# A decoder block on one core: the operand steps of the up products, the transposes and the first weight operands stand elsewhere in the program

## The chip, the cores and the metric

The kernel runs on one core of one Trainium2 chip. The metric is the device time of one launch in microseconds (us), as the median of the runs. Before the change it is 2093.09 us (three runs, 2091.72 to 2096.36). The profiled execution is another one: it took 2088.7 us, 2086.9 us from its first to its last instruction.

## What is computed

One layer of a hybrid decoder block over 1040 tokens (16 meta tokens and 1024 real ones) of 1024 channels, in float32. The part that the change touches is the end of the mixer and the start of the gated MLP:

```python
def block(h):
    mix = hybrid_mixer(rms_norm(h, g_pre_mix), ...)      # ends in: merged @ w_out
    h = h + rms_norm(mix, g_post_mix)
    ffn = conv_gated_mlp(rms_norm(h, g_pre_ffn), w_up_gate, conv_w_ffn, w_down)
    return (h + rms_norm(ffn, g_post_ffn))[:, 16:]

def conv_gated_mlp(xn, w_up_gate, conv_w_ffn, w_down):
    u, g = split(xn @ w_up_gate, 2)                      # 1024 x 5632
    u = causal_dwconv(u, conv_w_ffn)
    return (gelu(u) * g) @ w_down
```

So the norm of every token needs its whole row of `merged @ w_out`, and the up product needs the normalised rows with channels on the partitions, which is a transpose.

## The kernel before

Every float32 matmul is made of three passes: an operand is split into a high part (a cast, on ScalarE) and a low part (source less high part, on VectorE or GpSimd), and high x high, high x low and low x high are summed. `split` (L67) makes the two halves of an operand.

**Output projection (L921 to L938).** The tokens go in 9 blocks of 114 (QB), numbered 0 to 8. For each block `out_chunk` makes three chunks of up to 342 columns, 24 matmuls each, in one of three `po` banks (PSUM); ScalarE squares the chunk (L708) and VectorE multiplies it by the gain (L709). `post_block` then makes the first norm's root (`rstd_of`, L71: VectorE, one ScalarE square root, VectorE), the new row of h (L723), its square (L726), the second root and the normalised row xv (L728). Eight TensorE transposes of xv (L735) and two copies out of PSUM (L745 on ScalarE, L747 on VectorE) put the block into `xr`. The transposes of a block are kept in the list `to_transpose` and called after the third chunk of the next block.

**Operands of the up products.** The up product is a fast scheme over 2 x 2 blocks: seven products instead of eight, over token pairs (even tokens E, odd tokens O; the digit is the half of the channels). Its seven data operands are B11 = E1, T1 = O1 - E1, T2 = O2 - T1, B21 = E2, T3 = T2 - E1, B22 = O2 and T4 = E2 - T2, each split into high and low parts; the differences overwrite `xr`. The 514 pairs are worked in two halves (`HALF`: 258 and 256 pairs), because the first half needs only blocks 0 to 4. `x_early` makes B11, T1 and the sums of T2 and T3; `x_late` makes T2, B21, T3, B22 and T4. The low parts of B11, B21 and B22 are made on GpSimd, the others on VectorE. For the first half `x_early(0)` stands in block 6 and `x_late(0)` behind block 8; for the second half both stand behind the sixth product of the first set.

**Up products.** A set of `products` is seven groups of 12 matmuls in the order B11, T1, T2, B21, T3, B22, T4; ScalarE takes three snapshots of unfinished banks (L853, L856, L859), VectorE adds them in `evac_u` (L899). Pair 0 is worked as two sets, one for each half of the tokens (258 and 256 columns), then comes the gate pair as one set of 512 columns, and so on over 22 pairs. The weight operands of a pair (seven, from two raw tiles of 512 KB) come from `prep_pair`: ScalarE cast, GpSimd low part, and three VectorE sums. `prep0` is that of pair 0, `prep` that of the next one.

**Order.** The order in which instructions stand on each engine is set by a scheduler from the written order and from the waits, so it is not quite that of the code; each engine then works its own list strictly in order. The excerpts of the order below are from the built programs. TensorE's list at this joint was B11, T1 (first half), the transposes of block 8, then T2, B21, T3, B22, T4.

In the built program before, the operands are numbered: opB_13038 is B11, opT_13039 T1, opT_14199 T2, opB_14200 B21, opT_14201 T3, opB_14202 B22, opT_14203 T4. In the changed one opT_14168 is T2, opB_14167 B21, opT_14166 T3, opB_14258 B22, opT_14257 T4 (B11 and T1 keep theirs). 128x4x258 is an operand half for the first 258 pairs, 128x4x256 for the second.

## Time and profile before

| | us |
|---|---|
| median of 3 runs | 2093.09 |
| runs | 2091.72 to 2096.36 |
| profiled execution | 2088.7 |
| its span, first to last instruction | 2086.9 |
| TensorE busy | 1988.2 (95% of the span) |
| VectorE busy | 1070.9 (51%) |
| ScalarE busy | 851.7 (41%) |
| GpSimd busy | 908.1 (44%) |

TensorE (PE) is busy nearly throughout; of 40 slices of the span, the first, one from about 1357 us on and the last one fall short of nine tenths. In the timeline a row is the start, the duration, the engine, the line, the operation, what it writes and reads, and how often; in brackets stands how long the engine had been idle before it and what ended that. VectorE is DVE, ScalarE ACT, GpSimd POOL; SPq is the queue that issues transfers. Neighbouring matmuls overlap in the records, so the pace of TensorE is read from start to start.

### The profile page before, as it was taken

The page shows a single profiled execution, that of the slowest core. Times are in us where ns is not written, and L with a number is a line of the kernel's source. Part 1 is how long each engine was busy: PE and PEld are TensorE (multiplying, and loading weights), DVE is VectorE, ACT ScalarE, POOL GpSimd, SP SyncE. Part 2 cuts the span into 40 slices and gives each one's busy share as a digit, 9 for nine tenths or more (in the row PEclk, how much of TensorE's full clock was granted, in tenths as well). Part 3 has the DMA queues.
Part 4 walks back from the last instruction along what each step waited for, and adds up shares of the span by engine and source line. Part 5 has one row for each costly group of instructions (what it writes and reads, how often), then busy time and mean ns, then how long its engine had stood idle before and what let it go on. Part 6 is the DMA issues. An engine that isn't in the chain of part 4 may idle for free. (4 is left out here: it accounts for less than half of the span.)

```text
span 2086.9 us, 30864 instructions
## 1 busy us (share of the span) xinstructions
PE 1988.2 (95%) x12228; PEld 1858.4 (89%) x12228; DVE 1070.9 (51%) x1685; ACT 851.7 (41%) x1769; POOL 908.1 (44%) x765
## 2 busy tenths in 40 slices
PE   5999999999999999999999999969999999999997
PEld 4999999999999999999999999968998898878876
DVE  6455565655555565564341125774435444445547
ACT  4444454545454454544430123354344334321122
POOL 4443444434353444344122560155555655554353
PEclk9999999999999999999999999989999999999999
DMA  3111111111111101111475674302212222243223
GB/s 134 41 51 41 61 31 51 41 51 41 51 51 41 51 31 62 41 51 61 143 229 172 183 184 147 102 30 82 101 62 81 87 76 81 71 174 120 81 81 132
DMA packets 56030, 177.58 MB, mean 85 GB/s; under 512 B 12728, under 2 KB 12728, under 8 KB 55884
## 3 DMA queue, kind: packets, MB, share of 16 engines
q1 hardware_dynamic: 54732, 173.50, 25.7%
q8 instruction: 96, 1.57, 0.3%
q10 hardware_dynamic: 1152, 2.10, 0.3%
q14 instruction: 50, 0.41, 0.1%
HBM read 131.36 MB, written 44.21 MB: 84 GB/s over the span
## 5 line engine op out<-in xcount | busy, mean ns | idle before, releaser
L128 PE MATMUL mm<-xnT,whi 128*128 128x342 f32 (+2 forms) x1536 | 506.6, 330 | 5.1 <-ACT xnT L68 3.6
L129 PE MATMUL mm<-xnT,whi 128*128 128x342 f32 (+2 forms) x1536 | 493.8, 321 | 0.5 <-DVE xnT L69 0.5
L130 PE MATMUL mm<-xnT,wlo 128*128 128x342 f32 (+2 forms) x1536 | 492.2, 320 | 0.0
L338 POOL TENSOR_TENSOR be<-be,fl 114x127 f32<-114x127 f32 (+2 forms) x144 | 176.8, 1228 | 402.6 <-DVE fl L336 195.1
L128 PEld LDWEIGHTS mm<-xnT,whi 128*128 128x128 f32 x1536 | 289.8, 189 | 10.1 <-ACT xnT L68 4.2
L129 PEld LDWEIGHTS mm<-xnT,whi 128*128 128x128 f32 x1536 | 290.4, 189 | 2.1 <-DVE xnT L69 1.0
L130 PEld LDWEIGHTS mm<-xnT,wlo 128*128 128x128 f32 x1536 | 289.7, 189 | 0.0
L69 POOL TENSOR_TENSOR wlo<-raw,whi 128x1024 fp32r<-128x1024 f32 x80 | 205.7, 2572 | 189.9 <-ACT whi L68 189.9
L69 POOL TENSOR_TENSOR a_op<-raw,a_op 128x512 fp32r<-128x512 f32 (+1 forms) x134 | 185.7, 1400 | 96.7 <-ACT a_op L68 94.2
L336 DVE TENSOR_TENSOR_SCAN fl<-fl 114x128 f32<-114x128 f32 (+2 forms) x144 | 205.0, 1423 | 4.9
L69 DVE TENSOR_TENSOR al<-tp,ah 128x342 fp32r<-128x342 f32 (+4 forms) x288 | 126.9, 450 | 139.7 <-ACT ah L68 137.5
L68 ACT CAST ah<-tp 128x342 fp32r<-128x342 f32 (+4 forms) x288 | 113.1, 398 | 189.8 <-PE tp L372 181.9
L844 PE MATMUL st<-opT,a_op 128*128 128x258 f32 (+2 forms) x528 | 172.3, 326 | 15.0 <-DVE owork L899 7.9
L846 PE MATMUL st<-opT,a_op 128*128 128x258 f32 (+2 forms) x528 | 169.7, 321 | 0.0
L848 PE MATMUL st<-opT,a_op 128*128 128x258 f32 (+2 forms) x528 | 169.6, 321 | 0.0
L327 ACT ACTIVATE fl<-z 114x348 f32<-114x348 f32 (+10 forms) x240 | 111.5, 465 | 130.3 <-PE z L326 122.9
L68 ACT CAST a_op<-raw 128x512 fp32r<-128x512 f32 (+1 forms) x134 | 82.9, 628 | 161.5 <-DMA raw<-in_w_up_gate_dram 58.0
L1089 DVE TENSOR_TENSOR acc<-acc,st 128x512 f32<-128x512 f32 x144 | 98.4, 687 | 96.1 <-PE st L1084 96.1
L372 PE MATMUL tp<-ident,be 114*128 114x114 f32 x720 | 119.5, 263 | 25.6 <-DVE al L69 21.0
L846 PE MATMUL st<-opB,a_op 128*128 128x512 f32 (+2 forms) x396 | 127.6, 322 | 1.0 <-POOL opB L69 1.0
L844 PE MATMUL st<-opB,a_op 128*128 128x512 f32 (+2 forms) x396 | 127.4, 322 | 0.0
L848 PE MATMUL st<-opB,a_op 128*128 128x512 f32 (+2 forms) x396 | 127.3, 321 | 0.0
(164 smaller groups left out, 4374.3 us busy)
## 6 DMA issues: line engine op xcount, KB each, us to landing
raw<-in_w_in_dram SPq DMA_DIRECT2D x64, 512.0 KB
raw<-in_w_up_gate_dram SPq DMA_DIRECT2D x44, 512.0 KB
act_d<-owork SPq DMA_DIRECT2D x22, 512.0 KB
araw<-act_d SPq DMA_DIRECT2D x22, 512.0 KB
raw<-in_w_down_dram SPq DMA_DIRECT2D x22, 512.0 KB
y_d<-yy SPq DMA_DIRECT2D x8, 513.0 KB
ga_d<-gt SPq DMA_DIRECT2D x8, 513.0 KB
o_d<-ot SPq DMA_DIRECT2D x8, 513.0 KB
```

Of the source, the lines that this page charges most:

```text
L68: nc.scalar.copy(hi, src)
L69: (lo_engine or nc.vector).tensor_tensor(lo, src, hi.bitcast(F32), op=ALU.subtract)
L128: nc.tensor.matmul(ps, wh, xh, start=(kb == 0), stop=False)
L129: nc.tensor.matmul(ps, wh, xl, start=False, stop=False)
L130: nc.tensor.matmul(ps, wl, xh, start=False, stop=(kb == KB - 1))
L327: nc.scalar.activation(fl[:, c0:c0 + n], z, AF.Sigmoid, scale=-0.125)
L336: nc.vector.tensor_tensor_scan(fl[:, :nk][:, ::-1], fl[:, :nk][:, ::-1], fl[:, :nk][:, ::-1], 1.0, op0=ALU.mult, op1=ALU.min)
L338: nc.gpsimd.tensor_tensor(be[:, 0:nk - 1], be[:, 0:nk - 1], fl[:, 1:nk], op=ALU.mult)
L372: nc.tensor.transpose(tp[:n, QB * j:QB * (j + 1)], blocks[j][0][:, kb * P:kb * P + n], ident[:QB, :QB])
L844: nc.tensor.matmul(ps, wt[:, 0, k], xh, start=start and kb == 0, stop=False, skip_group_check=True)
L846: nc.tensor.matmul(ps, wt[:, 0, k], xl, start=False, stop=False, skip_group_check=True)
L848: nc.tensor.matmul(ps, wt[:, 1, k], xh, start=False, stop=stop and kb == 3, skip_group_check=True)
```

## The change

- The transposes of a block are called after the first chunk of the block after next (before: after the third chunk of the next block), as long as two are waiting. Block 7's transposes come after the second product of the first set, block 8's after the sixth, in the code.
- `x_early` and `x_late` are taken apart into `op_split` and `x_t1` to `x_t4` over ranges of pairs: R0 is the first half, R1 pairs 258 to 398, R2 399 to 513, RL both. For the first half B11, T1 and the sums of T2 and T3 stand in blocks 6 and 7; T2, B21 and T4's sum stand between the last matmuls of block 8 and its evacuation; T3 stands inside `post_block(8)`, in the two places where it waits for ScalarE; B22 and T4 stand after the third product. For the second half B11, and later T1, of R1 stand in block 8 and behind the third product, the rest after the sixth.
- Low parts of B11 (except R0), B21 and B22 (except RL) go from GpSimd to VectorE. Low parts of the merged input `mb` of blocks 6, 7 and 8 go from VectorE to GpSimd.
- The weight operands of pair 0 are asked for in blocks 2 to 5, 7 and 8, their raw tiles in block 0. The weights' low parts stay on GpSimd.
- Memory: `ones_up`, `tmp_s`, one row tile and the operand tiles move between pools; the pool `late` is opened in block 8, and `late2` holds T4 and B22.

```diff
@@ load_m
-        split(t[:, 0], t[:, 1], raw)
+        split(t[:, 0], t[:, 1], raw, nc.gpsimd if b > 5 else nc.vector)
...
@@ post_block
+    def post_block(b, ssq, between=(lambda: None, lambda: None)):
...
         r = rstd_of(osml, s0, QB)
+        between[0]()
         nc.vector.scalar_tensor_tensor(h, h, r, xv, op0=ALU.mult, op1=ALU.add)
...
         nc.scalar.activation(xv, h, AF.Square, accum_out=s2[:QB])
+        between[1]()
         r2 = rstd_of(osml, s2, QB)
...
+    def op_split(name, r, which, engine):
+        t = ops[name][:, :, :, r[0]:r[1]]
+        split(t[:, 0], t[:, 1], quarter(r, which), engine)
...
+    def x_t1(r):
+        sub(nc.vector, quarter(r, "O1"), quarter(r, "O1"), quarter(r, "E1"))
+    def x_t2(r):
+        sub(nc.vector, quarter(r, "O1"), quarter(r, "O2"), quarter(r, "O1"))
+    def x_t3(r):
+        sub(nc.vector, quarter(r, "E1"), quarter(r, "O1"), quarter(r, "E1"))
+    def x_t4(r):
+        sub(nc.vector, quarter(r, "E2"), quarter(r, "E2"), quarter(r, "O1"))
+    R0 = HALF[0]
+    R1, R2 = (258, 399), (399, NJ)
+    RL = (258, NJ)
...
+    def ahead(b, c):
+        if (b, c) == (0, 2):
+            load_pair(0)
+        elif 1 < b < 6 and c == 1:
+            next(prep0)
+        elif b == 6:
+            if c == 1:
+                op_split("B11", R0, "E1", nc.gpsimd)
+                x_t1(R0)
+            elif c == 2:
+                op_split("T1", R0, "O1", nc.vector)
+        elif b == 7:
+            if c == 1:
+                x_t2(R0)
+            elif c == 2:
+                x_t3(R0)
+                next(prep0)
+        elif b == 8:
+            if c == 0:
+                next(prep0)
+            elif c == 1:
+                op_split("B11", R1, "E1", nc.vector)
+                x_t1(R1)
...
         for c in range(3):
-            out_chunk(b, c, sums)
-            if b == 6 and c == 2:
-                x_early(0)
...
-        if to_transpose:
-            to_transpose.pop(0)()
-        post_block(b, sums)
+            ps = out_products(b, c)
+            if (b, c) == (8, 2):
...
+                op_split("T2", R0, "O1", nc.vector)
+                op_split("B21", R0, "E2", nc.vector)
+                x_t4(R0)
+            out_evac(b, c, ps, sums)
+            if c == 0 and len(to_transpose) > 1:
+                to_transpose.pop(0)()
+            ahead(b, c)
...
-        if k >= 1:
-            next(prep0, None)
-        if k == 5:
+        elif k == 1:
             to_transpose.pop(0)()
...
+        elif k == 2:
+            op_split("B22", R0, "O2", nc.vector)
+            op_split("T4", R0, "E2", nc.vector)
+            op_split("T1", R1, "O1", nc.vector)
+        elif k == 5:
+            to_transpose.pop(0)()
+            op_split("B11", R2, "E1", nc.vector)
+            x_t1(R2)
+            op_split("T1", R2, "O1", nc.vector)
+            x_t2(RL)
+            op_split("T2", RL, "O1", nc.vector)
+            op_split("B21", RL, "E2", nc.vector)
+            x_t3(RL)
+            op_split("T3", RL, "E1", nc.vector)
+            op_split("B22", RL, "O2", nc.gpsimd)
+            x_t4(RL)
+            op_split("T4", RL, "E2", nc.vector)
```

VectorE, from the evacuation of block 8's last chunk on, before (tmp_s and raw are the weight sums of pair 1; s, v and t belong to the root):

```order
L709 TENSOR_TENSOR row_13049<-po,g_post 114x340
L747 COPY xr<-tp 128x4x114
L721 TENSOR_REDUCE s_14163<-sums 114x1
L76 TENSOR_SCALAR v<-s_14163 114x1
L78 RECIPROCAL s<-s 114x1
L79 SCALAR_TENSOR_TENSOR t<-s,v 114x1
L80 TENSOR_SCALAR t<-t 114x1
L81 TENSOR_TENSOR s<-s,t 114x1
L723 SCALAR_TENSOR_TENSOR row_13049<-row_13049,s,xv_13047 114x1024
```

VectorE at the same place now:

```order
L712 TENSOR_TENSOR row_13048<-po,g_post 114x340
L770 TENSOR_TENSOR xr<-xr 128x1032
L724 TENSOR_REDUCE s_14177<-sums 114x1
L770 TENSOR_TENSOR opT_14166<-xr,opT_14166 128x4x258
L72 TENSOR_SCALAR v<-s_14177 114x1
L752 COPY xr<-tp 128x4x114
L74 RECIPROCAL s<-s 114x1
L830 TENSOR_TENSOR tmp_s<-raw 128x512
L75 SCALAR_TENSOR_TENSOR t<-s,v 114x1
L770 TENSOR_TENSOR raw<-raw 128x512
L76 TENSOR_SCALAR t<-t 114x1
L770 TENSOR_TENSOR raw<-tmp_s,raw 128x512
```

The step of T4's sum, T3's low part and the three weight sums, which stood ahead of or behind this piece before, now stand inside it, ahead of the new row of h (L727, the second row after these).

ScalarE from the same evacuation on, before (L708 squares the chunk, L77 is the root, L853 to L859 the snapshots):

```order
L708 ACTIVATE row_13049,sums<-po 114x340
L745 COPY xr<-tp 128x4x114
L77 ACTIVATE s<-v 114x1
L853 COPY snap<-st 128x258
L856 COPY snap<-st 128x258
L726 ACTIVATE xv_13047,s_14176<-row_13049 114x1024
```

ScalarE now:

```order
L711 ACTIVATE row_13048,sums<-po 114x340
L983 CAST opT_14166<-xr 128x4x258
L867 COPY snap<-st 128x258
L870 COPY snap<-st 128x258
L750 COPY xr<-tp 128x4x114
L873 COPY snap<-st 128x258
L73 ACTIVATE s<-v 114x1
L730 ACTIVATE xv_13046,s_14191<-row_13048 114x1024
L64 CAST opB_14258<-xr 128x4x258
```

The root of block 8 (L77, now L73) moved behind all three snapshots and behind the copy of block 7's transposes; the high part of B22 stands behind block 8's second root.

TensorE around the transposes of block 8, before:

```order
L848 MATMUL st<-opT_13039,a_op 128x258
L735 MATMUL tp<-ident,xv_13047 128x114 x5
L844 MATMUL st<-opT_14199,a_op 128x258
L735 MATMUL tp<-ident,xv_13047 128x114 x3
L844 MATMUL st<-opB_14200,a_op 128x258
```

TensorE around them now:

```order
L862 MATMUL st<-opT_14166,a_op 128x258
L740 MATMUL tp<-ident,xv_13046 128x114 x5
L858 MATMUL st<-opB_14258,a_op 128x258
L740 MATMUL tp<-ident,xv_13046 128x114 x3
L860 MATMUL st<-opB_14258,a_op 128x258
```

Block 8's transposes moved from behind T1's product to behind T3's; block 7's, which stood ahead of the first product, now stand behind T1's.

## Rows read from the trace of the kernel before

**Rows 1.** The page: span, and busy time of each engine.

```profile
span 2086.9 us, 30864 instructions
PE 1988.2 (95%) x12228; PEld 1858.4 (89%) x12228; DVE 1070.9 (51%) x1685; ACT 851.7 (41%) x1769; POOL 908.1 (44%) x765
```

**Rows 2.** Busy time by stretch: PE, weight loads, DVE, ACT, POOL, clock, DMA.

```profile
1245.00:1357.20 112.20, 107.87 (x699) 106.90 (x698) 72.89 (x154) 42.12 (x109) 16.16 (x10) 0.98 0.39 123
1357.20:1402.50 45.30, 28.51 (x183) 26.72 (x182) 34.68 (x38) 21.71 (x34) 23.42 (x10) 0.77 0.04 11
1402.50:1420.70 18.20, 16.89 (x75) 13.44 (x74) 12.13 (x10) 10.34 (x15) 10.50 (x9) 1.00 0.18 59
```

**Rows 3.** Timeline of TensorE: transposes of blocks 3 to 8, and restarts after waits.

```profile
1304.33 0.95 PE L735 MATMUL tp<-ident,xv 114*128 114x114 f32 x8
1316.40 0.94 PE L735 MATMUL tp<-ident,xv 114*128 114x114 f32 x8
1331.80 1.52 PE L735 MATMUL tp<-ident,xv 114*128 114x114 f32 x8 [2.76 <-DVE xv L728]
1345.02 0.94 PE L735 MATMUL tp<-ident,xv 114*128 114x114 f32 x8
1357.03 0.94 PE L735 MATMUL tp<-ident,xv 114*128 114x114 f32 x8
1367.11 1.19 PE L735 MATMUL tp<-ident,xv 114*128 114x114 f32 x5 [6.25 <-DVE xv L728]
1385.82 0.56 PE L844 MATMUL st<-opT,a_op 128*128 128x258 f32 x1 [4.81 <-DVE owork L899]
1402.71 0.40 PE L844 MATMUL st<-opB,a_op 128*128 128x512 f32 x1
1409.76 0.50 PE L844 MATMUL st<-opT,a_op 128*128 128x512 f32 x1 [1.31 <-ACT snap L853]
```

**Rows 4.** Timeline of TensorE, second token half: the pace at both clocks.

```profile
1389.60 0.41 PE L844 MATMUL st<-opB,a_op 128*128 128x256 f32 x1
1389.82 0.41 PE L846 MATMUL st<-opB,a_op 128*128 128x256 f32 x1
1390.18 0.28 PE L844 MATMUL st<-opT,a_op 128*128 128x256 f32 x1
1390.30 0.28 PE L846 MATMUL st<-opT,a_op 128*128 128x256 f32 x1
```

**Rows 5.** Timelines of ACT and DVE: block 8's chain to xv, a snapshot.

```profile
1357.22 0.46 ACT L708 ACTIVATE row<-po 114x340 f32<-114x340 f32 x1 [3.18 <-PE po L706]
1357.34 0.69 DVE L816 TENSOR_TENSOR tmp_s<-raw 128x512 f32<-128x512 f32 x1 [1.24 <-DMA raw<-in_w_up_gate_dram]
1359.52 0.51 DVE L709 TENSOR_TENSOR row<-po,g_post 114x340 f32<-114x340 f32 x1
1360.85 0.20 ACT L77 ACTIVATE s<-v 114x1 f32<-114x1 f32 x1 [2.65 <-DVE v L76]
1361.92 1.28 DVE L723 SCALAR_TENSOR_TENSOR row<-row,s,xv 114x1024 f32<-114x1024 f32 x1
1365.68 1.28 DVE L728 SCALAR_TENSOR_TENSOR xv<-row,s,g_pre 114x1024 f32<-114x1024 f32 x1
1373.99 0.38 ACT L859 COPY snap<-st 128x258 f32<-128x258 f32 x1 [0.47 <-PE st L848]
```

**Rows 6.** Timelines of DVE and POOL behind it: operand steps alone and side by side.

```profile
1369.91 1.24 DVE L69 TENSOR_TENSOR opT<-xr,opT 128x1032 fp32r<-128x1032 f32 x1 [2.95 <-ACT opT L68]
1371.09 15.96 POOL L69 TENSOR_TENSOR opB<-xr,opB 128x1032 fp32r<-128x1032 f32 x5 [16.76 <-PE tp L735]
1374.56 6.86 DVE L763 TENSOR_TENSOR xr<-xr 128x1032 f32<-128x1032 f32 x2
1384.91 1.09 DVE L899 TENSOR_TENSOR owork<-st,snap 128x258 f32<-128x258 f32 x3
```

**Rows 7.** Timeline of the transfer queue: the second raw tile of pair 1.

```profile
1353.11 0.35 SPq L800 DMA_DIRECT2D raw<-in_w_up_gate_dram  x1
```

More of the change, by code (lines that the diff above doesn't have):

```diff
@@ L673, in block_kernel @@
     ops = {name: early.tile([P, 2, 4, NJ], F32R, name=f"op{name}") for name in ("B11", "T1")}
-    tmp_s = early.tile([P, 512], F32, name="tmp_s")
     o_ctx = ctx.enter_context(ExitStack())
+    osml = o_ctx.enter_context(pool("osml", 4))
     ow = o_ctx.enter_context(pool("ow"))
-    osml = o_ctx.enter_context(pool("osml", 4))
     xvs = [pl.tile([P, D], F32, name=f"xv{i}") for i, pl in enumerate((early, ow))]
-    rws = [ow.tile([P, D], F32, name=f"row{i}") for i in range(2)]
+    rws = [pl.tile([P, D], F32, name=f"row{i}") for i, pl in enumerate((early, ow))]
+    tmp0 = ow.tile([P, 512], F32, name="tmp0")
     g_pre2 = ow.tile([P, D], F32, name="g_pre2")
@@ L808, in prep_pair @@
         got = a_ops[i] = {}
+        if i == 0:
+            tmp_s = tmp0
+        else:
+            tmp_s = shared.get("tmp")
+            if tmp_s is None:
+                tmp_s = shared["tmp"] = mpool.tile([P, 512], F32, name="tmp_s", tag="mb")
         def keep(name, src):
@@ L950, in bank_of @@
+            out_evac(b, c, ps, sums)
+            if c == 0 and len(to_transpose) > 1:
+                to_transpose.pop(0)()
+            ahead(b, c)
+        if b == 8:
+            t3, e1 = ops["T3"][:, :, :, R0[0]:R0[1]], quarter(R0, "E1")
+            post_block(b, sums, (lambda: nc.scalar.copy(t3[:, 0], e1),
+                                 lambda: sub(nc.vector, t3[:, 1], e1, t3[:, 0].bitcast(F32))))
+        else:
+            post_block(b, sums)
     def bank_of(pl, tag):
         return lambda: pl.tile([P, 512], F32, name="st", tag=tag)
-    first = products(0, *HALF[0], bank_of(ps_mm2, "mm"), evac_u(*HALF[0]))
@@ L954, in block_kernel @@
-    for k, _ in enumerate(first):
-        if k >= 1:
-            next(prep0, None)
-        if k == 5:
-            to_transpose.pop(0)()
-            x_early(1)
-            x_late(1)
+    for k, _ in enumerate(products(0, *HALF[0], bank_of(ps_mm2, "mm"), evac_u(*HALF[0]))):
+        if k == 0:
+            next(prep0)
+        elif k == 1:
+            to_transpose.pop(0)()
+            o_ctx.close()
+            late2 = late_ctx.enter_context(pool("late2", 1, "right"))
+            for name in ("T4", "B22"):
+                ops[name] = late2.tile([P, 2, 4, NJ], F32R, name=f"op{name}")
+        elif k == 2:
[15 more added lines that the diff above has]
+            op_split("T4", RL, "E2", nc.vector)
```

62 lines of the change are left out of this document (20 added, 42 removed).

## The prediction

> **What bounds the kernel now.** Read the page first: TensorE is busy for 95% of the span, no other engine for more than 51% [rows 1]. So a change of the order can only win where TensorE waits or runs slowly, and the stretches are compared next: through the output projection it is busy for 107.87 of 112.20 us at a clock of 0.98, but from there to the gate pair for 28.51 of 45.30 us at 0.77, and in the gate pair at 1.00 again [rows 2]. The change touches just these. Then the timeline of TensorE tells where the time goes [rows 3].
>
> Between undisturbed blocks transposes follow each other after 1316.40 - 1304.33 = 12.07 us. From 1316.40 to 1345.02, two blocks, it is 28.62 instead of 24.14: **4.5 us** lost. The wait itself is 2.76 us, for xv of block 5; the rest is the slow restart (eight transposes in 1.52 us instead of 0.94).
>
> I call 0 the moment at which block 8's last chunk ends (1357.03, where the transposes of block 7 begin). The gate pair begins at 1402.71, so at **45.7**. What must run in between is two sets of 84 matmuls at 0.12 us [rows 4], 20.2 us, and twice eight transposes, 1.9 us: 22.1. So **23.6 us** are lost, and two waits show why: 6.25 us for xv of block 8, then 4.81 us at VectorE's additions; after both the pace is 0.22 us a matmul instead of 0.12, which ends 4.2 us after the restart at 1385.82 (0.22 from 1389.60 to 1389.82, 0.12 from 1390.18 on) [rows 3, 4]. Last, 1.31 us in the gate pair, for a snapshot [rows 3].
>
> Why VectorE is late is in its own timeline: an operand step of 1032 elements takes 1.24 us alone and 6.86 / 2 = 3.43 us while GpSimd makes the B operands, five in 15.96 us, 3.2 each [rows 6].
>
> **The change part by part.**
>
> *Transposes a chunk later, operand steps of the first half spread.* A chunk is (12.07 - 0.94) / 3 = 3.7 us. Block 5's xv was 2.76 us late; its transposes are now asked for 3.7 us later, and in VectorE's list only one of the four long steps of the first half stands ahead of this xv. I take the whole 4.5 us; the ends are 0 and 4.5, since the same VectorE work stays in this block.
>
> *Reload of xv.* Its row tile is free a chunk later, so the transfer starts a chunk later. It has two chunks and the first root, about 10 us, and a 512 KB tile took 1353.11 to 1357.34, 4.2 us, from issue to use [rows 5, 7]: hidden, with some 6 us to spare. In the transfer queue only these reloads change places.
>
> *Weights of pair 0 in early blocks; mb on GpSimd.* As many instructions as before; VectorE is busy for 72.89 of these 112.20 us and GpSimd for 16.16 [rows 2]. That cover hides them: 0. What it costs without the cover is the first rival.
>
> *First half after block 8.* B11 and T1: 24 x 0.12 = 2.9; block 7's transposes to 3.8; T2, B21 and T3, 36 x 0.12 = 4.3, to 8.1. Their low parts stand in VectorE's list ahead of, or just behind, the last evacuation: five steps of 1.24 around 0, ready by about 5. TensorE need not wait before **8.1**.
>
> *Block 8's xv.* This is the price of the change. Its root now stands on ScalarE behind the third snapshot, which needs T2's product: 3.8 + 13 x 0.12 = 5.4, and 0.38 for the copy [rows 5]: 5.8 instead of 1360.85 - 1357.03 = 3.8. On VectorE the new row came 1.07 us after the root's start (1361.92). Now the three weight sums of pair 1 are threaded in between; they took 1357.34 to 1359.52, 2.2 us. If they fell wholly into the pauses of the root's small steps, nothing were added, if not at all, 2.2; the three are as long as the whole chain that they are threaded into, so I take 1.8. Row at 5.8 + 1.1 + 1.8 = 8.7. From the row's start to the first transpose it stays 1367.11 - 1361.92 = 5.2: **13.9**, where it was 10.1. So TensorE waits 5.8 us, about as long as the 6.25 before, only later: this wait isn't removed.
>
> *Restart.* As at the two restarts in the trace, at half clock for 4.2 us: eight transposes at 1.19 / 5 each are 1.9, eleven matmuls of B22 at 0.22 are 2.4: 18.2. Then T4 of the first and B11 of the second half at full clock.
>
> *Second half.* VectorE ends xv at about 13.8; the low parts of B22 and T4 to 16.2; the copy and the additions (1.09 for three [rows 6]), the last of which waits for B22's product, to 18.6. Then three steps of 115 pairs at 0.6, seven of 256 at 1.24, one addition of 0.4: 10.9, to 29.5. One GpSimd step, B22 of the second half, is left beside them; a step beside GpSimd took 3.43 instead of 1.24 [rows 6], so 2.2 more: 31.7. Ends of this: 0, if it hits a pause, and 4.4, if two steps are hit. The last product needs 1.4: gate pair at **33.1**, so 45.7 - 33.1 = 12.6 us gained.
>
> The SBUF — State Buffer page of the Trainium skill, in Who interferes with whom, says that a VectorE instruction with two SBUF inputs and a GpSimd one that reads SBUF exclude each other for a whole instruction, the loser standing still. The 3.43 beside 3.2 in the trace agree. By that rule a step that comes just after GpSimd's start would stand for all of the 3.2 instead of 2.2: an estimate of 2076.3 instead of the sum below.
>
> *Gate pair.* Its 1.31 us wait is for a snapshot behind the convolution's ScalarE work; the sets' last additions are now nearer to their products, so this may shrink. Between 0 and 1.3 I take 0.7.
>
> Sum: 4.5 + 12.6 + 0.7 = **17.8 us**. Against the profiled execution of 2088.7 this is 2070.9. That execution was 4.4 us under the median of the runs, so for the median 2093.1 - 17.8 = **2075.3**.
>
> **The rivals.**
>
> *VectorE becomes the bound in blocks 6 to 8.* Four long steps, 5.0 us, come into block 6, where VectorE has 72.89 / 112.20 x 12.07 = 7.8 us of work already (some of it these same steps), and GpSimd gets a B11 step of 3.2 and the mb splits, each of which holds VectorE. If that is over 12.07 us, block 5's transposes wait again (4.5 back) and block 8's row starts up to 4 us late: 2075.3 + 8.5 = 2083.8. For it: the 3.43. Against it: VectorE's evacuations have three banks of slack, and the transposes a chunk more.
>
> *The gain is handed back behind xv of block 8.* Everything of the second half hangs on it, and it comes 3.8 us later. If what follows took as long as before, 45.7 - 10.1 = 35.6, the gate pair would begin at 49.5, and with the 4.5 of block 5 the time would be 2092.4: no change. Against it: these 35.6 held five GpSimd steps with VectorE at 3.43; now one.
>
> *The joint is late for another reason* (the second raw tile of pair 1 waits for GpSimd's last weight step and comes after 5.8; T4's high part waits for VectorE's xv). Each us is paid once: up to 9 us, 2080 to 2088.
>
> *Slower: the clock stays at half.* TensorE now waits at 8.1 and is then fed step by step until 33. If the clock didn't return there, the gate pair's matmuls, about 20 us with one set, would take 20 us more and the next pair's as many. It decides from about 18 us of matmul time at half clock beyond the count above; through both pairs 40 - 17.8 = 22 us slower, 2115; through one, 2095. Against it: every restart in the trace came back, and the gate pair ran at 1.00 [rows 2].
>
> **How the numbers follow.** Chances: forecast 0.62 (2070 to 2080), VectorE as the bound 0.16, another late joint 0.09, handed back 0.07, clock 0.06. The range leaves out the last two and most of the third: 2068 (no GpSimd overlap, sums hidden, all of the gate's wait gone: -17.8 - 2.2 - 1.8 - 0.6 is 2070.7, and some 2 us of the runs' own spread) to 2084 (the first rival). A measurement of this kernel can tell about 0.2%, 4 us, from no change. Faster by more: 0.62 + 0.16 + 0.09 = 0.87; within: 0.07; slower: 0.06.
>
> **What would show it.** Right: no wait before the transposes in block 7, where 2.76 stood; one wait of 5 to 7 us between T3 and B22 of the first half, ended by xv; VectorE's steps at 1.24 us except at one GpSimd step; the gate pair 31 to 35 us after block 8's last chunk. Wrong: PE waits for VectorE in blocks 6 to 8; xv of block 8 later than 16; half clock in the gate pair; steps of 3 us on VectorE without GpSimd beside them.

## The result, and the profile after

The changed kernel takes **2079.67 us** (median of 11 runs, 2074.28 to 2085.38) against 2091.72 us for the kernel before, run beside it on the same chip: 12.05 us faster. Over all runs of both kernels the ratio is 0.9937 with a 95% interval of 0.9918 to 0.9955 (the two medians alone give 0.9942). The forecast was 2075.3, 17.8 us faster, with a range of 2068 to 2084. Its profiled execution has a time of 2075.06 and a span of 2073.3, 13.6 us under that of before.

The page's row of busy times holds little: the work is the same, TensorE's share is one point higher than in [rows 1].

```profile
PE 1985.7 (96%) x12228; PEld 1856.8 (90%) x12228; DVE 1071.2 (52%) x1689; ACT 850.4 (41%) x1771; POOL 903.3 (44%) x764
```

The stretches say more. The columns are those of [rows 2]: stretch, its length, busy time of TensorE, weight loads, VectorE, ScalarE and GpSimd (instructions in brackets), granted clock, DMA share and GB/s. The cuts are the start of the output projection, 0 as the prediction defined it (the end of block 8's last chunk, here 1348.03), block 8's transposes, the gate pair's first product, and a point in the gate pair.

```profile
1241.30:1348.03 106.73, 106.73 (x706) 106.49 (x705) 68.64 (x146) 38.77 (x101) 18.55 (x11) 1.00 0.39 116
1348.03:1368.60 20.57, 10.00 (x70) 9.46 (x69) 18.38 (x34) 11.39 (x27) 3.08 (x2) 0.83 0.30 87
1368.60:1390.73 22.13, 17.68 (x117) 16.85 (x118) 21.00 (x21) 13.22 (x19) 11.54 (x5) 0.85 0.02 6
1390.73:1408.00 17.27, 15.54 (x68) 12.32 (x67) 12.76 (x9) 10.12 (x16) 10.57 (x7) 1.00 0.19 62
```

The projection has TensorE busy throughout, at a clock of 1.00 where it was 0.98. The gate pair starts at 1390.73 - 1348.03 = 42.7 instead of 45.7: forecast was 33.1. So the joint gives 3.0 us and not 12.6. TensorE's waits there, in the timeline (start, duration, engine, line, operation; in brackets the idle time before and what ended it):

```profile
1327.73 0.94 PE L740 MATMUL tp<-ident,xv 114*128 114x114 f32 x8
1339.78 0.94 PE L740 MATMUL tp<-ident,xv 114*128 114x114 f32 x8
1355.13 1.75 PE L740 MATMUL tp<-ident,xv 114*128 114x114 f32 x8 [4.09 <-DVE xv L733]
1368.60 1.19 PE L740 MATMUL tp<-ident,xv 114*128 114x114 f32 x5 [6.48 <-DVE xv L733]
1377.56 0.38 PE L860 MATMUL st<-opB,a_op 128*128 128x256 f32 x1 [1.89 <-DVE opB L65]
1379.18 0.58 PE L860 MATMUL st<-opT,a_op 128*128 128x256 f32 x1 [1.12 <-DVE opT L65]
1389.20 0.39 PE L858 MATMUL st<-opT,a_op 128*128 128x256 f32 x1 [1.32 <-DVE owork L913]
1390.73 0.40 PE L858 MATMUL st<-opB,a_op 128*128 128x512 f32 x1
1403.74 0.50 PE L858 MATMUL st<-opT,a_op 128*128 128x512 f32 x1 [1.73 <-ACT snap L873]
```

Where 2.76 stood ahead of block 5's transposes in [rows 3] there is none now (1327.73), nor ahead of block 6's. But a wait is new ahead of block 7's (4.09), and block 8's, 13.9 by the forecast, come at 20.6. The one long wait between T3 and B22 is there, 6.48 us, ended by xv, but 6.7 us late. The reason is read in three timelines, of the transfer queue, GpSimd and VectorE:

```profile
1333.12 0.36 SPq L808 DMA_DIRECT2D raw<-in_w_up_gate_dram  x1
1334.46 0.27 SPq L728 DMA_DIRECT2D h_d<-row  x1
1334.82 0.28 SPq L722 DMA_DIRECT2D xv<-in_x_dram  x1
...
1331.81 1.29 POOL L65 TENSOR_TENSOR a_op<-raw,a_op 128x512 fp32r<-128x512 f32 x1 [3.93 <-ACT a_op L64]
...
1333.15 1.28 DVE L727 SCALAR_TENSOR_TENSOR row<-row,s,xv 114x1024 f32<-114x1024 f32 x1
1345.69 1.29 DVE L727 SCALAR_TENSOR_TENSOR row<-row,s,xv 114x1024 f32<-114x1024 f32 x1 [5.23 <-DMA xv<-in_x_dram]
1363.41 1.29 DVE L727 SCALAR_TENSOR_TENSOR row<-row,s,xv 114x1024 f32<-114x1024 f32 x1
```

The xv tile for block 7 is free when block 5's transposes end, 1327.73 + 0.94 = 1328.67. Its reload goes out at 1334.82: ahead of it in SP's list stand pair 1's raw tile, whose buffer GpSimd's weight step frees at 1331.81 + 1.29 = 1333.10, and block 6's row store, whose row is ready at 1333.15 + 1.28 = 1334.43. Then the load takes 1345.69 - 1334.82 = 10.9 us where a raw tile took 4.2 in [rows 5, 7]. VectorE stands 5.23 us, block 7's row is late, and block 8's behind it.

From the transposes to the gate pair it took 22.1, by the forecast 19.2. VectorE's and GpSimd's timelines there:

```profile
1374.04 3.46 DVE L65 TENSOR_TENSOR opB<-xr,opB 128x1024 fp32r<-128x1024 f32 x1
1377.42 1.70 DVE L65 TENSOR_TENSOR opT<-xr,opT 128x460 fp32r<-128x460 f32 x1
1383.93 2.32 DVE L65 TENSOR_TENSOR opT<-xr,opT 128x1024 fp32r<-128x1024 f32 x1
1386.50 1.98 DVE L65 TENSOR_TENSOR opT<-xr,opT 128x1024 fp32r<-128x1024 f32 x1
...
1373.78 2.63 POOL L65 TENSOR_TENSOR opB<-xr,opB 128x1024 fp32r<-128x1024 f32 x1 [20.66 <-ACT opB L64]
1376.43 2.20 POOL L65 TENSOR_TENSOR a_op<-tmp_s,a_op 128x512 fp32r<-128x512 f32 x1
1382.90 6.71 POOL L65 TENSOR_TENSOR a_op<-raw,a_op 128x512 fp32r<-128x512 f32 x3 [4.27 <-ACT a_op L64]
```

Four VectorE steps are held, not one: the first beside B22's low part, as foreseen, the others beside the low parts of pair 1's weights. TensorE stands for two of them (1.89 for opB and 1.12 for opT in its rows above).

Ahead of these stages and behind them 4.3 us lie between the two profiled executions (2.3 ahead of the projection, 2.0 from pair 2 on, both in favour of the changed kernel), in code that the change all but leaves alone. Ahead of the projection the profiles differ by far more than that without any edit there: it starts between 1240.9 and 1258.7 us (latest in before_later_tp, old_place and third_xv_dve, whose profiled executions are among the slowest of their runs). So the experiments are compared by stage, and for the whole by the ratio of their runs to those of the kernel before. The table gives, in us: length of the projection; block 8's transposes and gate pair, both counted from 0; the way between these two; the gate pair's length to pair 2's first product; pair 2's length to the next gate pair; the sum of projection, joint, gate pair and pair 2; the ratio to the kernel before.

| kernel | projection | transposes | way | gate at | gate pair | pair 2 | sum | ratio (interval) |
|---|---|---|---|---|---|---|---|---|
| before | 113.4 | 10.1 | 35.6 | 45.7 | 21.1 | 20.1 | 200.3 | 1 |
| after | 106.7 | 20.6 | 22.1 | 42.7 | 21.5 | 20.3 | 191.2 | .9937 (.9918 to .9955) |
| after_again | 108.7 | 22.9 | 23.1 | 46.0 | 21.2 | 20.2 | 196.1 | .9945 (.9926 to .9965) |
| before_later_tp | 107.3 | 14.4 | 36.9 | 51.3 | 19.9 | 20.1 | 198.6 | .9986 (.9967 to 1.0005) |
| old_place | 115.9 | 14.4 | 23.1 | 37.4 | 21.1 | 20.3 | 194.8 | .9975 (.9953 to .9997) |
| xv_on_act | 107.3 | 20.6 | 22.4 | 43.0 | 21.6 | 20.3 | 192.2 | .9957 (.9938 to .9975) |
| no_gpsimd_joint | 107.9 | 19.9 | 18.6 | 38.5 | 20.1 | 20.1 | 186.6 | .9933 (.9913 to .9953) |
| third_xv | 106.6 | 15.4 | 24.3 | 39.7 | 21.3 | 20.4 | 188.0 | .9949 (.9918 to .9980) |
| third_xv_2 | 106.7 | 16.8 | 25.9 | 42.7 | 19.9 | 20.3 | 189.5 | .9945 (.9923 to .9967) |
| third_xv_dve | 106.8 | 14.2 | 20.2 | 34.4 | 21.1 | 24.5 | 186.8 | .9926 (.9898 to .9954) |
| third_xv_dve_2 | 107.0 | 14.3 | 20.1 | 34.4 | 21.0 | 24.5 | 186.9 | .9912 (.9894 to .9931) |
| all_dve | 107.7 | 13.6 | 20.2 | 33.8 | 21.0 | 24.6 | 187.1 | .9905 (.9887 to .9924) |
| all_dve_2 | 106.6 | 13.6 | 20.2 | 33.7 | 21.7 | 24.5 | 186.6 | .9918 (.9900 to .9937) |
| ops_on_gpsimd | 107.9 | 22.5 | 24.4 | 46.9 | 21.3 | 20.3 | 196.4 | .9950 (.9933 to .9968) |

### The profile page after: what moved, and what is told of

Same layout as the page of the kernel before. It is cut to its first block, busy times and chain, and to the rows that moved or that the text cites. A ratio compares the mean times of both kernels' runs of the same rounds, so it can differ in the third digit from the quotient of the medians.

```text
span 2073.3 us, 30863 instructions
## 1 busy us (share of the span) xinstructions
PE 1985.7 (96%) x12228; PEld 1856.8 (90%) x12228; DVE 1071.2 (52%) x1689; ACT 850.4 (41%) x1771; POOL 903.3 (44%) x764
## 4 chain that ended last, share of the span: by engine, by line
PE 79%; DVE 9%; ACT 3%; issue 3%; POOL 3%; DMA 3%; DVEq 0%; SPq 0%; ACTq 0%; POOLq 0%
PE mm L124 13%; PE mm L125 13%; PE mm L126 12%; PE st L858 6%; PE st L860 6%; PE st L862 6%; PE tp L372 3%; PE st L1141 3%; PE st L1139 3%; PE st L1140 3%; PE av L362 2%; PE av L363 2%; PE z L326 2%; PE z L325 2%; POOL a_op L65 2%
## 5 line engine op out<-in xcount | busy, mean ns | idle before, releaser
L372 PE MATMUL tp<-ident,be 114*128 114x114 f32 x720 | 119.5, 263 | 25.6 <-DVE al L65 21.2
L860 PE MATMUL st<-opB,a_op 128*128 128x512 f32 (+2 forms) x396 | 127.3, 321 | 1.9 <-DVE opB L65 1.9
L1141 PE MATMUL st<-dt 128*128 128x512 f32 x320 | 125.4, 392 | 2.7 <-POOL dt L65 2.7
L858 PE MATMUL st<-opB,a_op 128*128 128x512 f32 (+2 forms) x396 | 127.3, 321 | 0.0
```

The source lines that it names most:

```text
L372: nc.tensor.transpose(tp[:n, QB * j:QB * (j + 1)], blocks[j][0][:, kb * P:kb * P + n], ident[:QB, :QB])
L858: nc.tensor.matmul(ps, wt[:, 0, k], xh, start=start and kb == 0, stop=False, skip_group_check=True)
L860: nc.tensor.matmul(ps, wt[:, 0, k], xl, start=False, stop=False, skip_group_check=True)
L1141: nc.tensor.matmul(ps, th, wl[:, c], start=False, stop=(j == len(fbs) - 1))
```

## The experiments

Theory A held that the late reload of xv keeps the joint back; theory B, that GpSimd's low parts do, by holding VectorE.

**xv_on_act.** The last two reloads are issued by ScalarE, right behind the transposes that free the tile.

```diff
-        else:
+        elif b < 7:
             nc.sync.dma_start(xv, x[t - 2:t - 2 + QB, :])
...
+            if b in (5, 6):
+                nc.scalar.dma_start(xv, x[t + 2 * QB - 2:t + 3 * QB - 2, :])
```

> The changed kernel, with the reloads of xv for blocks 7 and 8 issued from ScalarE's queue, right behind the copies out of the transposes that free the tile, instead of SP's queue. Times are counted from the end of block 8's last chunk; in the changed kernel the gate pair starts 42.7 us later. Theory A (the late reload of block 7 is what the missing gain hangs on): the reload is issued some 19 us before that point (13.2 in the changed kernel), lands some 11 us later, the new row of block 7 waits under 1 us for it (5.23), PE waits under 0.5 us before block 7's transposes (4.09), block 8's new row starts near 10 (15.4), its transposes near 15.5 (20.6), the gate pair near 37.5. Some 5 us less than the changed kernel: about 2074.5 us, 0.991 of the time before. Theory B (VectorE, held by GpSimd, is late anyway): the wait for the transfer goes, but the gate pair starts at 41 or later, and the ratio stays between 0.993 and 0.995.

Gate pair at 43.0: nothing moved. The timelines of ScalarE, VectorE and TensorE show that the experiment missed its aim:

```profile
1334.95 1.07 ACT L730 ACTIVATE xv<-row 114x1024 f32<-114x1024 f32 x1 [2.29 <-DVE row L727]
1336.34 0.58 ACTq L754 DMA_DIRECT2D xv<-in_x_dram  x1
...
1345.86 1.29 DVE L727 SCALAR_TENSOR_TENSOR row<-row,s,xv 114x1024 f32<-114x1024 f32 x1 [4.91 <-DMA xv<-in_x_dram]
...
1353.05 0.97 PE L740 MATMUL tp<-ident,xv 114*128 114x114 f32 x8 [1.71 <-DVE xv L733]
1368.93 1.18 PE L740 MATMUL tp<-ident,xv 114*128 114x114 f32 x5 [5.16 <-DVE xv L733]
```

ScalarE itself stood behind block 6's row, so the reload went out no sooner, and VectorE waited 4.91 for it. It says nothing for or against A, but two other things. From another engine's queue the load takes 1345.86 - 1336.34 = 9.5 us, so it isn't the queue that makes it long. The Trainium skill (page DMA: Bandwidth & Descriptors, section Issuing engines are not separate DMA queues) says that transfers of all issuers share the same 16 DMA engines; these 9.5 us agree. And block 7's wait shrank from 4.09 to 1.71 while block 8's transposes stayed at 20.6: that wait isn't on the way to the gate pair.

**old_place.** The transposes at the old place, everything else as changed.

```diff
-            if c == 0 and len(to_transpose) > 1:
+            if c == 2 and to_transpose:
                 to_transpose.pop(0)()
...
         elif k == 1:
-            to_transpose.pop(0)()
```

> The changed kernel with the transposes of each block back at the place of before, behind the next block's last chunk. Both theories: the out projection gets back its wait before block 5's transposes (about 2.5 us) and its restart, 111 to 113.5 us instead of 106.7. Theory A (late reload of xv of block 7): the tile is free some 8 us earlier and its reload stands ahead of the weight tile of pair 1 in SP's list, so block 7's row does not wait (5.23 in the changed kernel) and the gate pair starts 34 to 38 us behind block 8's last chunk (42.7): in sum 2077 to 2081 us, 0.992 to 0.995. Theory B (VectorE is late anyway): the gate pair stays at 42 or later, and the time is 2084 to 2087 us, 0.996 to 0.998.

The joint came out as A says: the reload is in time, block 8's transposes stand at 14.4 (13.9 in the prediction), the gate pair at 37.4. The projection pays for it, more than expected, and the ratio stays above what was expected (TensorE's timeline, a row cut off at the window's end):

```profile
1344.98 0.42 PE L740 MATMUL tp<-ident,xv 114*128 114x114 f32 x1 [5.97 <-DVE xv L733]
```

Block 5's transposes wait 5.97 us, twice the 2.76 of [rows 3], since four long operand steps now stand ahead of that block's xv in VectorE's list; the projection takes 115.9, and the whole gains 0.25%.

**no_gpsimd_joint.** No GpSimd step beside the second columns: the low parts of pair 0's S4 and A22 and of all of pair 1's weights become ScalarE copies of the source (their subtraction is left out), and B22's last low part goes to VectorE.

```diff
-            split(t[:, 0], t[:, 1], src, nc.gpsimd)
+            if i == 1 or (i == 0 and name in ("S4", "A22")):
+                nc.scalar.copy(t[:, 0], src); nc.scalar.copy(t[:, 1], src)
+            else: split(t[:, 0], t[:, 1], src, nc.gpsimd)
...
-            op_split("B22", RL, "O2", nc.gpsimd)
+            op_split("B22", RL, "O2", nc.vector)
```

> The changed kernel without GpSimd in the joint: the low parts of S4 and A22 of pair 0 and of all of pair 1 are written as a copy by ScalarE (the subtraction is left out), and the low part of B22 for the second columns is made on VectorE. Theory B (GpSimd holds VectorE, and VectorE sets the joint): the VectorE steps beside GpSimd fall back to their own durations (second B21 3.46 to 1.24 us, two scalings of block 7 from 1.26 and 1.23 to 0.2, T1, T3 and T4 of the second columns from 1.70, 2.32 and 1.98 to 0.63, 1.23 and 1.23), some 7 us in sum less 1.2 for B22: the gate pair starts near 37.5 us behind block 8's last chunk (42.7), and the time is about 2074.5 us, 0.991 of before. Rival (theory A alone: what is late is late by the reload, and the held steps have slack): the wait of 5.23 us stays, the transposes of block 8 stay near 20, the gate pair stays at 41 or later and the ratio at 0.993 to 0.995.

```profile
1354.86:1374.75 19.89, 11.03 (x71) 10.16 (x69) 16.56 (x34) 12.43 (x29) 0.00 (x0) 0.83 0.30 90
1374.75:1393.31 18.56, 16.54 (x117) 15.55 (x118) 17.47 (x22) 15.77 (x24) 0.00 (x0) 0.91 0.02 7
```

The two stretches (columns as above) are 0 to block 8's transposes and on to the gate pair. With GpSimd silent (0.00) the second is 18.6 instead of 22.1; the first is 19.9 instead of 20.6, since the reload is still late. Each theory holds a part of the delay; that the two add up is shown by third_xv_dve below.

**third_xv.** A alone, by other means: three xv tiles take turns, so that block 7's reload waits for no transposes of block 5.

```diff
-    xvs = [pl.tile([P, D], F32, name=f"xv{i}") for i, pl in enumerate((early, ow))]
+    xvs = [pl.tile([P, D], F32, name=f"xv{i}") for i, pl in enumerate((ow, ow, early))]
...
-        xv = xvs[b % 2][:QB]
+        xv = xvs[b % 3][:QB]
```

> The changed kernel with three tiles for xv instead of two. The lists of VectorE and of TensorE stay as they are; on SP's queue the reload for block 7 now stands right behind block 5's row and ahead of the weight tile of pair 1, and it needs no transposes to end. Times are counted from the end of block 8's last chunk (gate pair at 42.7 in the changed kernel). Theory A (the late reload): the transfer lands before block 7's row step is due, so its 5.23 us of waiting go, VectorE's list runs on 5 us earlier, PE's wait of 4.09 us before block 7's transposes goes, block 8's row starts near 10.5 (15.4), its transposes near 15.5 (20.6), the gate pair near 37.5; some 5 us less than the changed kernel, 0.990 to 0.992 of the time before. Theory B (VectorE is late anyway, by its work and by GpSimd): the gate pair stays at 41 or later, the ratio at 0.993 to 0.996, as the run with the reload on ScalarE's queue had it, in which the reload was in fact issued no earlier (ScalarE stood behind block 6's row).

```profile
1324.44 0.28 SPq L722 DMA_DIRECT2D xv<-in_x_dram  x1
...
1347.03 1.28 DVE L727 SCALAR_TENSOR_TENSOR row<-row,s,xv 114x1024 f32<-114x1024 f32 x1
...
1369.95 0.42 PE L740 MATMUL tp<-ident,xv 114*128 114x114 f32 x1 [6.49 <-DVE xv L733]
```

Here 0 is 1354.55. The reload goes out 30.1 us ahead of it instead of 13.2, block 7's row waits for nothing, and block 8's transposes stand at 15.4, as expected. The gate pair comes at 39.7, not 37.5: 2.2 us are given back on the way, where GpSimd still holds VectorE (24.3 us at a clock of 0.80; 22.1 at 0.85 in the changed kernel). The ratio, .9949, lies where theory B had it.

**third_xv_dve.** third_xv with B's part too, computing everything: the low parts of pair 0's A22, of pair 1's weights and of the last B22 on VectorE.

```diff
-            split(t[:, 0], t[:, 1], src, nc.gpsimd)
+            split(t[:, 0], t[:, 1], src, nc.vector if i == 1 or (i, name) == (0, "A22") else nc.gpsimd)
...
-            op_split("B22", RL, "O2", nc.gpsimd)
+            op_split("B22", RL, "O2", nc.vector)
```

> The kernel with three xv tiles, and besides the low parts of A22 of pair 0, of all of pair 1 and of B22 for the second columns made on VectorE instead of GpSimd; nothing is left out. If GpSimd's steps hold VectorE's by more than they take there (holds of some 7 us in the joint against 1.2 us for B22 and six steps of 0.69, four of them ahead of the gate pair): transposes of block 8 to gate pair in 20 us (22.1; 18.6 in the run without GpSimd), the gate pair near 35.5, the wait of 1.73 us in the gate pair under 1, the ratio 0.988 to 0.991. If VectorE pays as much for the added steps as it gains: gate pair at 37 to 39, the same time as with three tiles alone.

Transposes at 14.2, way 20.2, gate pair at 34.4, where the prediction had 13.9, 19.2 and 33.1. Both causes taken away, its count of the joint stands. But the gate pair is no shorter (its wait, now for VectorE, is 1.09 us; under 1 was expected), the ratio misses what was expected, and pair 2 takes 24.5 us instead of 20.3, in all four profiles of this kind (third_xv_dve and all_dve, twice each). Stretch, TensorE and ScalarE of all_dve_2 show it:

```profile
1403.06:1427.55 24.49, 21.87 (x170) 21.66 (x169) 5.83 (x11) 7.09 (x15) 12.38 (x11) 0.93 0.41 129
...
1408.72 0.49 PE L858 MATMUL st<-opT,a_op 128*128 128x258 f32 x1 [2.62 <-ACT snap L867]
...
1407.78 0.62 ACT L64 CAST a_op<-raw 128x512 fp32r<-128x512 f32 x1 [7.05 <-DMA raw<-in_w_up_gate_dram]
```

ScalarE stands 7.05 us at the raw tile of the pair after (3.99 in the changed kernel), TensorE at the snapshot behind it, and then it runs for a while at the lower clock (0.93 over the stretch). The tile goes out 23.1 us behind the gate pair's start (20.1 in the changed kernel), and the two tiles ahead of it at 6.2 (2.0), when VectorE has made the last low parts of pair 1; that the one follows from the other is likely, but no run shows it. So 4.2 of the 8 us that the gate pair starts earlier are handed back one stage on.

**third_xv_dve_2**, the same kernel once more:

> Again the kernel with three xv tiles and the low parts of A22, of pair 1 and of the second B22 on VectorE, beside the changed kernel. Theory (reload and GpSimd's holds are what is missing): gate pair at 33.5 to 35 us (34.2 in the first run, 42.7 in the changed kernel), some 8 us less than the changed kernel, 0.9895 to 0.992 of the time before. Rival: what the stage gains is given back behind it (the first run's profile was 5 us longer behind the gate pair), and the time is within 3 us of the changed kernel's.

```profile
1349.64:1363.74 14.10, 7.96 (x69) 7.79 (x68) 12.25 (x24) 5.23 (x13) 0.00 (x0) 0.87 0.10 32
1363.74:1383.84 20.10, 18.07 (x117) 16.66 (x118) 18.12 (x24) 13.84 (x19) 0.00 (x0) 0.83 0.02 7
...
1370.28 1.22 DVE L65 TENSOR_TENSOR opB<-xr,opB 128x1024 fp32r<-128x1024 f32 x1
```

(The first stretch begins 0.2 us behind 0.) The joint repeats, the ratio is within what was expected, and the step of 3.46 above takes 1.22.

**before_later_tp.** The other half of the change alone: the kernel before, with the transposes later.

```diff
+            if c == 0 and len(to_transpose) > 1:
+                to_transpose.pop(0)()
...
-        if to_transpose:
-            to_transpose.pop(0)()
...
-        if k == 5:
+        if k in (1, 5):
             to_transpose.pop(0)()
```

> The kernel before with the later place of the transposes alone (behind the first chunk of the block after next; block 7's behind the first two products of the joint). The out projection loses its wait of 2.76 us before block 5's transposes, the restart behind it and one set of transposes that goes to the joint: 106.5 to 109 us instead of 113.5. The joint takes one set of transposes more and keeps its old operand steps on GpSimd: gate pair at 45.5 to 48 us (45.5). Together 3 to 6 us less than before, ratio 0.997 to 0.9985. If the later place is what opens the joint's gain, the gate pair comes under 44 and the ratio under 0.996.

The projection gains 6.1 us and the joint loses 5.6; the ratio doesn't differ from 1. The timelines of the queue, VectorE and TensorE:

```profile
1362.69 0.36 SPq L800 DMA_DIRECT2D raw<-in_w_up_gate_dram  x1
...
1371.18 0.69 DVE L816 TENSOR_TENSOR tmp_s<-raw 128x512 f32<-128x512 f32 x1 [5.76 <-DMA raw<-in_w_up_gate_dram]
...
1380.42 1.18 PE L735 MATMUL tp<-ident,xv 114*128 114x114 f32 x5 [10.57 <-DVE xv L728]
```

VectorE stands 5.76 us at pair 1's raw tile, which lands late. It is the second rival's outcome (gate pair at 49.5, no gain; 45.5 to 48 was expected here) by what the third rival names, a late second raw tile of pair 1: it goes out 3.3 us ahead of 0, as before (3.9), but it is used 8.5 us later instead of 4.2, with a reload of xv issued 3.7 us ahead of it. With old_place it gives the change's two halves: .9986 and .9975 apart, .9937 and .9945 together. The later transposes take the wait out of the projection, and the spread operand steps shorten the joint; neither does the other's part.

**after_again.** The changed kernel a second time, to see how far its stages repeat.

> The changed kernel itself, beside the three others on the same chip. All theories: out projection 106.5 to 107.5 us, gate pair 42 to 43.5 us behind block 8's last chunk, 0.993 to 0.996 of the time before.

The projection took 108.7 and the gate pair stood at 46.0, both outside what was expected. The reload was issued at 1338.63, and VectorE waited longer for it:

```profile
1338.63 0.28 SPq L722 DMA_DIRECT2D xv<-in_x_dram  x1
1351.31 1.28 DVE L727 SCALAR_TENSOR_TENSOR row<-row,s,xv 114x1024 f32<-114x1024 f32 x1 [7.04 <-DMA xv<-in_x_dram]
...
1374.21 1.18 PE L740 MATMUL tp<-ident,xv 114*128 114x114 f32 x5 [6.31 <-DVE xv L733]
```

Over the profiles of the changed kernel, xv_on_act and third_xv, in which VectorE's list between the two rows takes 17.7 to 17.9 us, the two go together: no wait for the reload (third_xv) puts block 8's transposes at 15.4, 4.91 and 5.23 at 20.6, 7.04 at 22.9. So the joint of the changed kernel varies by 3 us with a transfer, and a difference of that size between two single profiles is no finding.

**third_xv_2.** third_xv once more, to see what A is worth in the time.

> Again the kernel with three xv tiles alone. Theory (block 8's transposes start 15.2 us behind block 8's last chunk, plus the time that block 7's row waits for its reload; that is 5.23 and 7.04 us in the two profiles of the changed kernel, none here): transposes of block 8 at 15 to 15.7, gate pair at 39 to 40.5, GpSimd's holds in the second columns unchanged (second B21 some 3.4 us); 3 to 6 us less than the changed kernel, 0.9915 to 0.9935 of the time before. Rival: the time is that of the changed kernel, 0.9937 to 0.995, and the stage's gain is lost behind it.

Transposes at 16.8, gate pair at 42.7, later than expected, though block 7's row waits for nothing: VectorE's list to block 8's row took 19.2 us, 1.69 of it a wait for ScalarE, and the way 25.9 at a clock of 0.76. Against after's .9937 and .9945, third_xv's .9949 and .9945 show no gain: the earlier reload alone moves the transposes by 4 to 8 us, but in the time nothing of it can be told apart.

**all_dve.** third_xv_dve, and the low parts of the last mixing tiles and of the first B11 on VectorE as well. No GpSimd step but two of pair 0's weights is left beside the projection's last blocks and the joint.

```diff
-        split(t[:, 0], t[:, 1], raw, nc.gpsimd if b > 5 else nc.vector)
+        split(t[:, 0], t[:, 1], raw, nc.vector)
...
-                op_split("B11", R0, "E1", nc.gpsimd)
+                op_split("B11", R0, "E1", nc.vector)
```

> The last kernel, and besides the low parts of the attention operand of blocks 6 to 8 and of the first B11 on VectorE, so that GpSimd holds nothing in blocks 6 to 8 but two weight steps. Theory (VectorE's list in the joint runs without a gap, so that an earlier start of it is worth its length): block 7's row step starts 2 to 3 us earlier (7.7 us ahead of block 8's last chunk now), block 8's transposes at 11 to 12.5 (14.1), the gate pair at 31 to 33 (34.2), the ratio 0.988 to 0.991. Rival: the four steps added to VectorE in blocks 5 to 7 make the xv of blocks 5 and 6 late, PE waits 2 us or more before their transposes, and the out projection takes 108.5 to 111 us; nothing is won.

Block 8's transposes come at 13.6, the gate pair at 33.8 (11 to 12.5 and 31 to 33 were expected): block 7's row starts 1.8 us earlier than in third_xv_dve, but VectorE's list to block 8's row takes 1.1 us more. The gate pair's own length stays at 21.0, and pair 2 hands back as much as in third_xv_dve. Ratio .9905, the best of all.

**all_dve_2**, the same kernel again:

> Again the kernel with three xv tiles and no low part on GpSimd in blocks 6 to 8 and the joint but the two weight steps. As in its first run: gate pair at 33 to 34.5 us, gate pair itself 18.5 to 20.2 us long, 0.989 to 0.992 of the time before, 8 to 11 us less than the changed kernel.

All stages repeat within 1.1 us (the gate pair takes 21.7, not the 18.5 to 20.2 expected); ratio .9918. The kernel's two ratios lie under the changed kernel's two, though not all the intervals are apart: 2071.8 and 2072.2 against 2079.7 and 2078.5 us.

**ops_on_gpsimd.** The other direction: the B operands that the change brought to VectorE go back to GpSimd, the rest stays as changed.

```diff
-                op_split("B11", R1, "E1", nc.vector)
+                op_split("B11", R1, "E1", nc.gpsimd)
...
-                op_split("B21", R0, "E2", nc.vector)
+                op_split("B21", R0, "E2", nc.gpsimd)
...
```

(and so for the first B22, the second B11 and the second B21)

> The changed kernel with five operand steps back on GpSimd, as before the change: the low parts of B11 for the second columns (two), of B21 (two) and of the first B22. SP's list is the same. If a GpSimd step holds VectorE's for its length (2.5 us for 1032 columns against 1.2 on VectorE): VectorE is held 9 to 11 us and freed of 4.7, the gate pair starts at 46 to 50 us (42.7), the ratio is 0.996 to 0.999. If not (the change of engine was needless, only the order helps): VectorE loses 4.7 us of work in the joint, the gate pair starts at 38 to 41, the ratio is 0.991 to 0.993.

```profile
1362.82 2.98 DVE L65 TENSOR_TENSOR opT<-xr,opT 128x564 fp32r<-128x564 f32 x1
...
1362.04 3.16 POOL L65 TENSOR_TENSOR opB<-xr,opB 128x1032 fp32r<-128x1032 f32 x1 [0.23 <-ACT opB L64]
```

VectorE's step of 564 elements, 0.73 alone, takes 2.98 beside GpSimd's 3.16. The gate pair comes at 46.9, in the expected range. Its reload is waited for as long as in the first profile of the changed kernel (5.22 and 5.23 us), where the gate pair came at 42.7; but in after_again it came at 46.0, and the ratio, .9950, is that of the changed kernel (.9937 and .9945) within its interval and lower than expected. That the B operands went to VectorE can't be shown to be worth anything in the time: five of GpSimd's steps are moved, but pair 1's weights still hold VectorE.

## Why the prediction was right and wrong

The sign and the range were right; the sum failed by its largest term. In the profiled executions 17.8 were forecast and 13.6 measured: +9.6 for the joint, -2.2 for the projection, +1.1 for the gate pair, -4.3 in stages that the change doesn't touch. That the time came out inside the range is in part luck: in the stages that it was added up from the first profile gained 9.3 us and the second 4.3, and the range's upper end had been set by a rival (VectorE in blocks 6 to 8) that isn't what happened.

*Blocks, 4.5.* Right in kind, too small: no wait before block 5's transposes, and the projection is 6.7 us shorter in the first profile, 4.7 in the second (6.1 with the transposes alone). The 4.5 counted what two blocks lost against undisturbed ones; the row on the whole stretch had 112.20 - 107.87 = 4.3 us idle and, besides, a clock of 0.98 [rows 2], which is 1.00 now.

*Weights of pair 0 and mb, 0.* Right for the projection: TensorE waits for nothing in the blocks. Not for the joint, since pair 1's raw tile and GpSimd's weight steps come into it by the two steps below.

*Reload of xv, "hidden, with some 6 us to spare".* **This step failed.** It gave the reload about 10 us and a landing of 4.2. The issue was taken as a chunk later, because "in the transfer queue only these reloads change places": the reload went out 23.7 us ahead of 0 before (1333.35), and 13.2 ahead of it now, 10.5 us later, not 3.7. Of these, 4.3 come from the later end of block 5's transposes (a chunk and 0.6 more); the rest is 1334.82 - 1328.67 = 6.15 us of standing in SP's list behind a raw tile that waits for GpSimd and a row store that waits for VectorE. In the kernel before the reload stood ahead of that raw tile:

```profile
1333.35 0.27 SPq L719 DMA_DIRECT2D xv<-in_x_dram  x1
1338.09 0.36 SPq L800 DMA_DIRECT2D raw<-in_w_up_gate_dram  x1
```

And the landing was taken from a row with little else in flight (last section); behind a raw tile and a row store it took 10.9. Between issue and need there were 5.6 us, so VectorE stood 5.23. third_xv shows what this was worth at block 8's transposes: 20.6 - 15.4 = 5.2 (3.8 by third_xv_2).

*Block 8's xv at 13.9.* The terms stand once the reload is there and GpSimd's steps are gone from the row's path, or the transposes are at the old place: 13.6 to 14.4 in the five profiles of old_place, third_xv_dve and all_dve (15.4 and 16.8 in third_xv's two). From the row's start to the transposes it was 1368.60 - 1363.41 = 5.2, as forecast. What the prediction lacked is the path to the row: VectorE's list has no gap to speak of from block 7's row to block 8's, 1363.41 - 1345.69 = 17.7 us in the changed kernel, and as long in third_xv. So each us that block 7's row is late goes to block 8's in full. In third_xv_dve the list takes 1.1 us less: GpSimd doesn't hold block 7's root there (2.1 us, last section), and VectorE has two weight steps of 0.7 more. That gives 14.2 and not 15.4.

*Second half, "one GpSimd step ... 2.2 more".* **This step failed too.** The rows above are longer than alone by 3.46 - 1.24 = 2.2, 1.70 - 0.63 = 1.1, 2.32 - 1.23 = 1.1 and 1.98 - 1.23 = 0.75: 5.1 instead of 2.2. The 2.9 that it was short are as much as the 22.1 - 19.2 measured; that the steps are the cause is shown by the runs without them (18.6 and 20.1 to 20.2). The prediction followed the operand steps that the change moves and forgot that pair 1's weights, which it doesn't touch, stay on GpSimd and now fall beside VectorE's. Its upper end, two steps (4.4), was too low as well. So 6.7 (5.2 for the reload, most of the rest for block 7's root) and 2.9 here are the 9.6 of the joint. The size of single steps fits the page that the prediction cites (SBUF — State Buffer of the Trainium skill, Who interferes with whom), by which the later of two such instructions stands still until the other ends: 3.46 beside 2.63 and 2.20. The count of the steps was wrong.

*Gate pair, 0.7.* Wrong: the wait for the snapshot is 1.73 instead of 1.31. ScalarE's timeline shows what the snapshot stands behind:

```profile
1402.58 0.62 ACT L64 CAST a_op<-raw 128x512 fp32r<-128x512 f32 x1 [2.65 <-DVE raw L770]
1403.11 0.58 ACT L873 COPY snap<-st 128x512 f32<-128x512 f32 x1
```

a cast of a weight sum that VectorE made late. Where GpSimd's low parts are left out, TensorE's longest wait there shrinks to 0.31 (no_gpsimd_joint, gate pair 20.1). Where VectorE makes them, another comes in its place, of 1.01 to 1.74 us for VectorE's additions, and the gate pair takes 21.0 to 21.7. The cast and the snapshot weren't put the other way round by an experiment.

*The rivals.* VectorE as the bound was half right: it is late in blocks 6 to 8, but TensorE waits only at block 7's transposes, and this wait isn't on the path (xv_on_act). "Handed back" is what happens when the transposes alone are moved (gate pair at 51.3). "Late for another reason" is what happened, by a candidate that wasn't in its list. Half clock didn't come: the gate pair ran at 1.00.

What stays open: how much of the ratio each half of the delay is worth. In the joint the reload costs 4 to 5 us and GpSimd's steps some 4, but with the steps on VectorE pair 2 hands 4.2 back: to the next gate pair the changed kernel takes 191.2 and 196.1 us, third_xv 188.0 and 189.5, third_xv_dve and all_dve 186.6 to 187.1. In the ratios only the last two come out under the changed kernel, by 0.1 to 0.4%, with intervals that for the most part overlap; by the stages third_xv should have come out nearly as low.

## What to carry to other kernels

A transfer has two times, when its buffer comes free and when its queue's list lets it go; a step that is moved by one place should be looked up in the issuing engine's list, with what each transfer ahead of it waits for. Price a load by a row in which as much is in flight as there will be. When work leaves GpSimd, count what stays on it in the new stretch, not only what was moved. And follow a gain into the next stage: the joint that begins the gate pair 8 us earlier meets a raw tile that isn't there yet.

## What the runs showed that was not expected

Small VectorE steps pay for GpSimd in full. In block 7's second root of the changed kernel (VectorE's timeline; the third row, for comparison, is the root's first step, ahead of GpSimd's):

```profile
1349.89 1.26 DVE L75 SCALAR_TENSOR_TENSOR t<-s,v 114x1 f32<-114x1 f32 x1
1351.90 1.23 DVE L77 TENSOR_TENSOR s<-s,t 114x1 f32<-114x1 f32 x1
1348.20 0.15 DVE L72 TENSOR_SCALAR v<-s 114x1 f32<-114x1 f32 x1 [0.67 <-ACT xv L730]
```

Steps of one element a partition, 0.22 and 0.16 us alone, take 1.26 and 1.23 while GpSimd runs (1349.72 to 1351.14 and 1351.46 to 1353.12; each ends as GpSimd's instruction does), 2.1 us more together, in the list without a gap on which all of the second half hangs.

The reload took about as long as three transfers in turn. The raw tile (512 KB), the row store and the reload (456 KB each) were done 1345.69 - 1333.12 = 12.6 us after the first was issued, 1.46 MB at 116 GB/s, in after_again at 101; the raw tile of [rows 5, 7] took 4.2 us, 124 GB/s (not quite alone: in these 4.2 us 170 GB/s were moved in all). So the reload's 10.9 us are little more than its turn behind the other two. What held the three to this rate no run shows; the DMA engines were busy for a share of 0.40 in this stretch.
